# Weaving background steps twice per weight chunk, with scores and transposes of p in separate steps

## The chip, the core and the metric

One core of a Trainium2 chip runs one encoder block on 512 tokens of width 1024. The metric is the device time of the core in microseconds (us). The engines are named as in the profile: PE is TensorE (PEld its weight loads), DVE is VectorE, ACT is ScalarE, POOL is GpSimd, SP is SyncE.

## What is computed

One layer: a half-step SwiGLU, a mixer that joins a two-way RG-LRU with a neighbourhood attention, an output projection, and a second half-step SwiGLU. All of it is float32. The part around the change is the mixer:

```python
x = x + FFN_RES * _swiglu(_rmsnorm(x, norm_ffn1), w_ffn1_gu, w_ffn1_down)
h = _rmsnorm(x, norm_mix)
xr, gr, q, k, v, ga, gb = jnp.split(h @ w_in, splits, axis=-1)
xc = _centred_dwconv(xr, conv_w, conv_b)
y_lru = (rglru_forward(xc) + rglru_backward(xc)) * jax.nn.gelu(gr)
q = _rmsnorm(q, q_norm) * HEAD_DIM ** -0.5        # per head of 64
k = _rmsnorm(k, k_norm)
y_att = _neighbourhood_attention(q, k, v, rel_pos_bias)   # 8 x 16 window on an 8 x 64 grid
x = x + (sigmoid(ga) * y_lru + sigmoid(gb) * y_att) @ w_out
x = x + FFN_RES * _swiglu(_rmsnorm(x, norm_ffn2), w_ffn2_gu, w_ffn2_down)
```

## The kernel before

Every float32 product is made of three matmuls on operands that are cut into a high and a low part: high by high, high by low, low by high (`mm3`, and the same three lines in `tok_group`). Weights come in chunks of 128 x 1024 (`load_w`): SP issues the load, ACT casts the high part (L120), DVE subtracts to get the low part (L123), both with high priority. A chunk feeds 24 matmuls of 512 columns.

The mixer runs as one stream of such chunks: 8 for the LRU input (`xr`), then six token groups of 4 chunks (q, k, v of heads 0 to 7, then q, k, v of heads 8 to 15; `tok_group`), then 24 chunks of gates in three families of 8 (`gates`), then 8 chunks of the output projection. These streams accumulate in the four PSUM banks of the pool `acc`.

Everything else of the mixer is background work in two lanes of Python generators. `lanes["lru"]` holds two RG-LRU jobs (`lru`, four tiles of 128 channels each). `lanes["att"]` holds two attention jobs (`heads(0)` and `heads(1)`, eight heads each). `weave(rate)` adds a rate to a lane's account and emits one step of the generator for each whole unit in it. It is called once behind each chunk, with the rates of `RATE` for the stage: "xr", "t0" (first three token groups), "t1" (next three, when `heads(0)` is in the lane), "g" (gates, when `heads(1)` has been added). `until` empties a lane as far as a gate needs it.

A job of `heads` has these steps: the root and reciprocal of the q and k norms (L755, L756); the scaling of q (L761); the scaling of k (L761); `start(0)`, which transposes the first q and k tiles (L770, L772); then ten steps i = 0 to 9 over eight units (four pairs of heads, two halves each). Step i emits `scores` of unit i (12 matmuls L796 into two PSUM tiles of the pool `aux`; DVE adds the bias and takes the maximum, L806; ACT takes the exponential, L809; DVE scales, L815), for odd i from 3 on `apply` of an earlier pair (32 matmuls L834), for even i up to 4 `start` of the next pair, and then `turn` of unit i-1: eight transposes of p (L823), four into each of two `aux` tiles, which ACT copies out (L825). The pool `aux` has four PSUM banks. `scores` takes two, `start` two, each half of `turn` one and `apply` one; the LRU gates use them too.

The order within each engine's queue is made by a planner from the program: the program's order is the priority, and an instruction whose inputs its model finds ready may go ahead of earlier ones that are not. `after(i, prev)` tells it to place i behind prev; it makes no wait on the chip.

Of the kernel before, what the change touches and what calls it, by code (L numbers as in the profile page):

```python
# [11 lines left out]
AF = mybir.ActivationFunctionType  # L12
# [7 lines left out]
KT = D // P  # L20
# [38 lines left out]
ATT_LAG = 1, 2  # L59

RATE = {
    "xr": {"lru": 4, "att": 0.0},
    "t0": {"lru": 3, "att": 0.0},
    "t1": {"lru": 2, "att": 0.75},
    "g": {"lru": 3, "att": 0.75},
}


# [1 line left out]
def block_kernel(ctx: ExitStack, tc, a, out):  # L70
    nc = tc.nc
# [7 lines left out]
    dram = ctx.enter_context(tc.tile_pool(name="dram", bufs=1, space=bass.MemoryType.DRAM))  # L79

    uid = [0]

    def nm(s):
        uid[0] += 1
        return f"{s}_{uid[0]}"
# [3 lines left out]
    def big_t(dt=F32, shape=(P, T), n="b"):  # L89
        return big.tile(list(shape), dt, tag="big", bufs=NBIG, name=nm(n))  # L90

    def pair_t():
        return big.tile([P, 2, T], F32, tag="pair", bufs=4, name=nm("pair"))

    def acc_t():
        return acc.tile([P, T], F32, tag="acc", name=nm("acc"))
# [37 lines left out]
    def load_w(src, n, act=True):  # L134
        raw = raw_t()
        H, L = hl_t()
        s = slice(0, n)
        ld = nc.sync.dma_start(raw[:, s], src[:, s])
        if nld[0] < 8:
            tc.keep_in_program_order(ld)  # L140
        nld[0] += 1
        with tc.high_priority():
            split(raw[:, s], H[:, s], L[:, s], act)
        return H, L

    def mm3(ps, wh, wl, xh, xl, first, last, skip=False):
        nc.tensor.matmul(ps, wh, xh, start=first, stop=False, skip_group_check=skip)  # L147
        nc.tensor.matmul(ps, wh, xl, start=False, stop=False, skip_group_check=skip)  # L148
        nc.tensor.matmul(ps, wl, xh, start=False, stop=last, skip_group_check=skip)  # L149

    def feat_chunk(src, nk, xh, xl, ps, k0, ktot, act=True):
        H, L = load_w(src, nk * P, act)
        for k in range(nk):
            s = slice(k * P, (k + 1) * P)
            kk = k0 + k
            mm3(ps, H[:, s], L[:, s], xh[kk], xl[kk], kk == 0, kk == ktot - 1)


    def make_xg(gcol, tag):
        xh, xl = [], []  # L160
        for k in range(KT):
            xh.append(xpool.tile([P, T], F32R, tag=f"xh{k}", name=nm("xh")))
            xl.append(xpool.tile([P, T], F32R, tag=f"xl{k}", name=nm("xl")))
        ssum = xpool.tile([P, T], F32, tag="ssum", name=nm("ssum"))

        def one(k):
            g = small[:, gcol + k : gcol + k + 1]
            x = xres[k]
            nc.scalar.activation(xh[k], x, AF.Copy, scale=g)
            return nc.vector.scalar_tensor_tensor(xl[k], x, g, xh[k].bitcast(F32), ALU.mult, ALU.subtract)  # L170

        def square(k):
            x = xres[k]
            if k == 0:
                nc.scalar.activation(ssum, x, AF.Square)
            else:
                sq = big_t(n="xsq")
                nc.scalar.activation(sq, x, AF.Square)
                nc.vector.tensor_tensor(ssum, ssum, sq, ALU.add)

        return xh, xl, ssum, one, square
# [24 lines left out]
    def after(i, prev):  # L206

        i, prev = getattr(i, "ins", i), getattr(prev, "ins", prev)
        tc.add_manual_dep(i, prev.name, mybir.DependencyInfo(
            mybir.DependencyClass.NoSync, mybir.DependencyReason.DATA), reason="order")  # L210


    mark = {}

    def sub(out_, in0, in1, neg=False):

# [271 lines left out]
    def weave(rate):  # L488
        for ln, n in rate.items():
            q = lanes[ln]  # L490
            due[ln] += n
            while due[ln] >= 1 and q:
                try:
                    next(q[0])
                    due[ln] -= 1
                except StopIteration:
                    q.pop(0)
            if not q:
                due[ln] = 0.0
# [6 lines left out]
    xh, xl, ssum, one, square = make_xg(C_G1, "a")  # L506
# [53 lines left out]
    xh, xl, ssum = nxt["v"][:3]  # L560
# [45 lines left out]
    def conv(f, ps, r):  # L606
        xp = big.tile([P, T + 4], F32, tag="xp", bufs=2, name=nm("xp"))
        nc.gpsimd.memset(xp[:, 0:2], 0.0)
        nc.gpsimd.memset(xp[:, T + 2 : T + 4], 0.0)
        with tc.high_priority():  # L610
            nc.vector.tensor_tensor(perm(xp[:, 2 : T + 2]), blk(ps), blk(r), ALU.mult)
        y = big_t(n="xc")
        w = lambda k: small[:, C_CW + f * 4 + k : C_CW + f * 4 + k + 1]
        nc.scalar.activation(y, xp[:, 0:T], AF.Identity, scale=w(0), bias=small[:, C_CB + f : C_CB + f + 1])
        for k in range(1, CONV_W):
            mark["xr"] = nc.vector.scalar_tensor_tensor(y, xp[:, k : k + T], w(k), y, ALU.mult, ALU.add)
        xc[f] = y
# [61 lines left out]
    rb = None  # L679
    for f in range(KT):  # L680
        ps = acc_t()
        feat_chunk(a["wxr"][f], KT, xh, xl, ps, 0, KT)
        if f == 0:
            rb, rcol, vx = rstd(ssum)
            epsv = const.tile([P, NCB], F32, name="epsv")
            nc.vector.tensor_scalar(epsv, vx, EPS, None, ALU.mult)
        conv(f, ps, rb)
        weave(RATE["xr"])
        if (f + 1) % LRU_F == 0:
            lanes["lru"].append(lru(range(f + 1 - LRU_F, f + 1)))  # L690
# [4 lines left out]
    def tok_group(w, hf):  # L695
        pss = [acc_t() for _ in range(NCB)]
        for kp in range(4):
            H, L = load_w(a["wqkv"][w * 2 + hf, kp], 1024)
            for j in range(NCB):
                tj = slice(j * P, (j + 1) * P)  # L700
                for k in range(2):
                    kk = kp * 2 + k
                    s = slice(k * T, (k + 1) * T)
                    nc.tensor.matmul(pss[j], xh[kk][:, tj], H[:, s], start=kk == 0, stop=False)  # L704
                    nc.tensor.matmul(pss[j], xl[kk][:, tj], H[:, s], start=False, stop=False)  # L705
                    nc.tensor.matmul(pss[j], xh[kk][:, tj], L[:, s], start=False, stop=kk == KT - 1)  # L706
            if kp < 3:
                weave(RATE[phase[0]])
        return pss
# [31 lines left out]
    def bias(g):  # L741

        for hp in range(2):
            bms[g, hp] = tiny.tile([P, 3, 2 * P], F32, tag="bm", bufs=4, name=nm("bm"))
            ld = nc.gpsimd.dma_start(bms[g, hp], a["rpb"][g * 2 + hp])
            if g == 0:
                after(ld, mark["xr"])

    def heads(hf, raws, st):

        rq = tiny.tile([P, 2, NCB, 8], F32, tag="rq", name=nm("rq"))
        for w in range(2):
            for j in range(NCB):
                nc.vector.tensor_scalar(rq[:, w, j, :], st[:, w, j, :], 1.0 / HD, epsv[:, j : j + 1], ALU.mult, ALU.add)
        nc.scalar.activation(rq, rq, AF.Sqrt)  # L755
        nc.vector.reciprocal(rq, rq)  # L756
        yield
        for w in range(2):
# [93 lines left out]
        for i in range(len(units) + LC):  # L852
            if i < len(units):
                fi, n2 = units[i]
                last = scores(fi, n2)
                if i >= LC and units[i - LC][1]:
                    apply(units[i - LC][0], last)
                if n2 == 0:
                    if fi < 3:
                        start(fi + 1)  # L860
                    if hf * 4 + fi + 1 < KT:
                        bias(hf * 4 + fi + 1)
            if 0 <= i - LB < len(units):
                for hp in range(2):
                    turn(*units[i - LB], hp)
            if len(units) <= i < len(units) + LC and units[i - LC][1]:
                apply(units[i - LC][0])
            yield

    att = [None] * KT  # L870
    phase = ["t0"]
# [9 lines left out]
    def gates(w, fs, fn, scale=1.0):  # L881
        q = [pair_t() for _ in range((len(fs) + 1) // 2)]
        for i, f in enumerate(fs):
            ps = acc_t()
            feat_chunk(a["wg3"][w * KT + f], KT, xh, xl, ps, 0, KT, f % 2 == 0)
            with tc.high_priority():
                nc.vector.tensor_tensor(q[i // 2][:, i % 2], ps, rb, ALU.mult)
            weave(RATE[phase[0]])
        for i, t in enumerate(q):
            n = min(2, len(fs) - 2 * i)  # L890
            nc.scalar.activation(t[:, :n], t[:, :n], fn, scale=scale)
        return [(f, q[i // 2][:, i % 2]) for i, f in enumerate(fs)]
# [13 lines left out]
    for fs in GB_BATCH:  # L906
        for f, t in gates(2, fs, AF.Tanh, 0.5):
# [4 lines left out]
            L = big_t(F32R, n="yl")  # L912
# [9 lines left out]
    for m in range(KT):  # L922
        nc.sync.dma_start(xres[m], xd[m])
        ps = acc_t()
# [10 lines left out]
    xh, xl, ssum = nxt["v"][:3]  # L935
# [84 lines left out]
```

## Time and profile before

| | |
|---|---|
| median of 3 runs | 1131.18 us (1131.16 to 1131.39) |
| profiled execution | 1131.25 us, span 1129.1 us |
[...]
| PE busy | 1122.3 us (99% of the span) |
| DVE, ACT, POOL busy | 837.7, 594.0, 19.2 us |
| mixer stage | about 358 to 787 us of the span |

Busy time says that an engine had something in it. As matmuls are pipelined, a busy PE can still lose time between the starts of two matmuls. So the places of loss are read from the start times of a timeline of PE, and what caused them from the timelines of DVE and ACT at the same place.

### The profile page before, as it was taken

How to read it: one execution, taken by the hardware profiler on the slowest of the kernel's cores; microseconds unless marked ns; L12 is line 12 of the kernel's file. 1: busy time of each engine (PE TensorE's matmuls, PEld its weight loads, DVE VectorE, ACT ScalarE, POOL GpSimd, SP SyncE). 2: the span in 40 equal slices, each digit the busy share in tenths (PEclk: the TensorE clock that was granted, in tenths of full speed). 3: DMA queues.
4: the chain of work that ended last, by engine and by line, in shares of the span. 5: the costliest groups of instructions: out<-in, count | busy, mean ns of one | idle time of the engine just before them, and what ended most of it. 6: DMA issues, size and time to landing. Idle time of an engine off the chain costs nothing.

```text
span 1129.1 us, 17245 instructions
## 1 busy us (share of the span) xinstructions
PE 1122.3 (99%) x6867; PEld 992.8 (88%) x6867; DVE 837.7 (74%) x1294; ACT 594.0 (53%) x896; POOL 19.2 (2%) x52
## 2 busy tenths in 40 slices
PE   9999999999999999999999999999999999999998
PEld 7899999988888888888788888888999999998887
DVE  7888888894736798797865576858688888894552
ACT  8554554563624595985564254656445445464340
POOL 0000000000000000010110000000000000000000
PEclk9999999999999999999999999999999999999999
DMA  8242333443433342353453332355133333253321
GB/s 267 90 130 77 116 109 95 133 142 99 131 93 112 94 159 84 113 162 103 133 155 103 93 104 84 111 170 187 56 90 118 94 110 115 90 170 96 130 76 38
DMA packets 43697, 130.69 MB, mean 116 GB/s; under 512 B 5984, under 2 KB 8544, under 8 KB 43616
## 3 DMA queue, kind: packets, MB, share of 16 engines
q1 hardware_dynamic: 39744, 119.36, 33.6%
q0 software_dynamic: 3296, 9.97, 2.8%
q8 instruction: 54, 0.88, 0.3%
q10 hardware_dynamic: 576, 0.26, 0.1%
q14 instruction: 27, 0.22, 0.1%
HBM read 121.17 MB, written 8.39 MB: 115 GB/s over the span
## 4 chain that ended last, share of the span: by engine, by line
PE 97%; DVE 1%; ACT 1%; issue 0%; DMA 0%; ACTq 0%; DVEq 0%
PE acc L267 29%; PE acc L147 11%; PE acc L148 11%; PE acc L149 11%; PE aux L267 5%; PE aux L147 4%; PE aux L148 4%; PE aux L149 4%; PE acc L705 4%; PE acc L704 4%; PE acc L706 4%; PE aux L823 1%; PE aux L834 1%; PE aux L796 1%; PE acc L380 1%; PE acc L382 1%
## 5 line engine op out<-in xcount | busy, mean ns | idle before, releaser
L120 ACT ACTIVATE wh<-wraw 128x1024 fp32r<-128x1024 f32 (+3 forms) x242 | 240.9, 999 | 331.8 <-PE acc L267 95.9
L123 DVE TENSOR_TENSOR wl<-wraw,wh 128x1024 fp32r<-128x1024 f32 (+3 forms) x254 | 291.3, 1150 | 137.2 <-ACT wh L120 136.6
L267 PE MATMUL acc<-s,wh 128*128 128x256 f32 x1216 | 220.5, 283 | 0.0
L267 PEld LDWEIGHTS acc<-s,wh 128*128 128x128 f32 x1216 | 189.7, 192 | 0.0
L267 PE MATMUL acc<-s,wl 128*128 128x256 f32 x608 | 172.1, 283 | 0.0
L147 PE MATMUL acc<-xh,wh 128*128 128x512 f32 x304 | 120.1, 395 | 0.0
L148 PE MATMUL acc<-xl,wh 128*128 128x512 f32 x304 | 119.0, 392 | 0.0
L149 PE MATMUL acc<-xh,wl 128*128 128x512 f32 x304 | 118.9, 391 | 0.0
L267 PEld LDWEIGHTS acc<-s,wl 128*128 128x128 f32 x608 | 116.7, 192 | 0.0
L267 PE MATMUL acc<-xh,wl 128*128 128x256 f32 x304 | 86.0, 283 | 0.0
L267 PE MATMUL acc<-xl,wh 128*128 128x256 f32 x304 | 86.0, 283 | 0.0
L267 PE MATMUL acc<-xh,wh 128*128 128x256 f32 x304 | 86.0, 283 | 0.0
L704 PE MATMUL acc<-wh,xh 128*128 128x512 f32 x192 | 75.2, 392 | 0.0
L705 PE MATMUL acc<-wh,xl 128*128 128x512 f32 x192 | 74.8, 390 | 0.0
L706 PE MATMUL acc<-wl,xh 128*128 128x512 f32 x192 | 74.8, 389 | 0.0
L301 DVE TENSOR_TENSOR wraw<-wraw,pair 128x1024 f32<-128x1024 f32 x57 | 69.6, 1220 | 0.8
L147 PE MATMUL aux<-hh,wh 128*128 128x512 f32 (+1 forms) x181 | 69.9, 386 | 0.0
L148 PE MATMUL aux<-hl,wh 128*128 128x512 f32 (+1 forms) x181 | 69.9, 386 | 0.0
L149 PE MATMUL aux<-hh,wl 128*128 128x512 f32 (+1 forms) x181 | 69.9, 386 | 0.0
L149 PE MATMUL acc<-hh,wl 128*128 128x512 f32 (+1 forms) x176 | 67.9, 386 | 0.0
L148 PE MATMUL acc<-hl,wh 128*128 128x512 f32 (+1 forms) x176 | 67.9, 386 | 0.0
L147 PE MATMUL acc<-hh,wh 128*128 128x512 f32 (+1 forms) x176 | 67.9, 386 | 0.0
(203 smaller groups left out, 2196.9 us busy)
## 6 DMA issues: line engine op xcount, KB each, us to landing
wraw<-wqkv SPq DMA_DIRECT2D x24, 512.0 KB, 3.6
wraw<-wg SPq DMA_DIRECT2D x24, 512.0 KB, 3.6
wraw<-w1d SPq DMA_DIRECT2D x22, 512.0 KB, 3.6
wraw<-w2d SPq DMA_DIRECT2D x22, 512.0 KB, 3.6
pair<-w2s SPq DMA_DIRECT2D x20, 512.0 KB, 3.6
wraw<-w2s SPq DMA_DIRECT2D x20, 512.0 KB, 3.6
wraw<-w1s SPq DMA_DIRECT2D x18, 512.0 KB, 3.7
pair<-w1s SPq DMA_DIRECT2D x18, 512.0 KB, 3.6
```

What stands on the lines that cost most here:

```text
L120: nc.scalar.activation(H, raw, AF.Copy)
L123: nc.vector.tensor_tensor(L, raw, H.bitcast(F32), ALU.subtract)
L147: nc.tensor.matmul(ps, wh, xh, start=first, stop=False, skip_group_check=skip)
L148: nc.tensor.matmul(ps, wh, xl, start=False, stop=False, skip_group_check=skip)
L149: nc.tensor.matmul(ps, wl, xh, start=False, stop=last, skip_group_check=skip)
L267: nc.tensor.matmul(o, w_[:, c], x_, start=first and m + k == 0 and w_ is H and x_ is xh_, stop=m + k == 4 and w_ is L, skip_group_check=True)
L301: nc.vector.tensor_tensor(t, t, o, ALU.add)
L380: nc.tensor.matmul(pre[i], w[i][1][:, s], xh[k], start=k == 0, stop=False)
L382: nc.tensor.matmul(pre[i], w[i][1][:, s], xl[k], start=False, stop=False)
L704: nc.tensor.matmul(pss[j], xh[kk][:, tj], H[:, s], start=kk == 0, stop=False)
L705: nc.tensor.matmul(pss[j], xl[kk][:, tj], H[:, s], start=False, stop=False)
L706: nc.tensor.matmul(pss[j], xh[kk][:, tj], L[:, s], start=False, stop=kk == KT - 1)
```

## The change

The rates of the LRU lane are halved, and `weave` is called a second time in the middle of each chunk of the mixer's stream: behind half of the k steps of a chunk in `feat_chunk` (new argument `mid`, given for the xr chunks and the gates), and behind two of the four token blocks in `tok_group`. The rate of the attention lane stays at 0.75 per call, so it is doubled per chunk. In `heads` a `yield` is put between `scores` (with `apply` or `start`) and `turn`, so that each of the ten steps becomes two. The root of the q and k norms is placed behind the last matmul that was emitted before it (`mark["mm"]`).

```diff
 RATE = {
-    "xr": {"lru": 4, "att": 0.0},
-    "t0": {"lru": 3, "att": 0.0},
-    "t1": {"lru": 2, "att": 0.75},
-    "g": {"lru": 3, "att": 0.75},
+    "xr": {"lru": 2, "att": 0.0},
+    "t0": {"lru": 1.5, "att": 0.0},
+    "t1": {"lru": 1, "att": 0.75},
+    "g": {"lru": 1.5, "att": 0.75},
 }
...
-        nc.tensor.matmul(ps, wl, xh, start=False, stop=last, skip_group_check=skip)
+        mark["mm"] = nc.tensor.matmul(ps, wl, xh, start=False, stop=last, skip_group_check=skip)
...
-    def feat_chunk(src, nk, xh, xl, ps, k0, ktot, act=True):
+    def feat_chunk(src, nk, xh, xl, ps, k0, ktot, act=True, mid=None):
...
             mm3(ps, H[:, s], L[:, s], xh[kk], xl[kk], kk == 0, kk == ktot - 1)
+            if mid is not None and k == nk // 2 - 1:
+                weave(mid)
...
-        feat_chunk(a["wxr"][f], KT, xh, xl, ps, 0, KT)
+        feat_chunk(a["wxr"][f], KT, xh, xl, ps, 0, KT, mid=RATE["xr"])
...
-                    nc.tensor.matmul(pss[j], xh[kk][:, tj], L[:, s], start=False, stop=kk == KT - 1)
+                    mark["mm"] = nc.tensor.matmul(pss[j], xh[kk][:, tj], L[:, s], start=False, stop=kk == KT - 1)
+                if j == 1:
+                    weave(RATE[phase[0]])
...
-        nc.scalar.activation(rq, rq, AF.Sqrt)
+        after(nc.scalar.activation(rq, rq, AF.Sqrt), mark["mm"])
...
                     if hf * 4 + fi + 1 < KT:
                         bias(hf * 4 + fi + 1)
+            yield
             if 0 <= i - LB < len(units):
                 for hp in range(2):
                     turn(*units[i - LB], hp)
...
-            feat_chunk(a["wg3"][w * KT + f], KT, xh, xl, ps, 0, KT, f % 2 == 0)
+            feat_chunk(a["wg3"][w * KT + f], KT, xh, xl, ps, 0, KT, f % 2 == 0, RATE[phase[0]])
```

## Rows read from the trace of the kernel before

**Rows 1.** The page: busy time, share of the span and instructions of each engine.
```profile
PE 1122.3 (99%) x6867; PEld 992.8 (88%) x6867; DVE 837.7 (74%) x1294; ACT 594.0 (53%) x896; POOL 19.2 (2%) x52
```

**Rows 2.** Waits of PE's weight loads: who for whom, total us, times, longest.
```profile
PEld aux L823 <- DVE nmx L806: 2.6, 4, 1.0
```

**Rows 3.** Timeline: start, us, engine, line, out<-in, count; late transposes of p.
```profile
547.18 0.39 PE L704 MATMUL acc<-wh,xh 128*128 128x512 f32 x1
548.15 0.66 PE L823 MATMUL aux<-ident,p 128*128 128x128 f32 x4 [0.58 <-DVE nmx L806]
...
673.13 0.39 PE L147 MATMUL acc<-xh,wh 128*128 128x512 f32 x1
673.63 0.66 PE L823 MATMUL aux<-ident,p 128*128 128x128 f32 x4
...
696.29 0.40 PE L149 MATMUL acc<-xh,wl 128*128 128x512 f32 x1
696.93 0.66 PE L823 MATMUL aux<-ident,p 128*128 128x128 f32 x4 [0.24 <-DVE nmx L806]
...
727.74 1.46 PE L823 MATMUL aux<-ident,p 128*128 128x128 f32 x8
...
735.49 0.42 PEld L834 LDWEIGHTS aux<-PT,v 128*64 128x64 f32 x8 [0.17 <-issue]
```

**Rows 4.** Timeline of DVE ahead of the first of them.
```profile
543.17 1.90 DVE L761 TENSOR_TENSOR qk<-qk,rq 128x512 f32<-128x512 f32 x3
...
546.19 1.22 DVE L123 TENSOR_TENSOR wl<-wraw,wh 128x1024 fp32r<-128x1024 f32 x1
547.32 0.42 DVE L806 CUSTOM_DVE_ANT_0 so<-aux,bm 128x256 f32<-128x256 f32 x1
```

**Rows 5.** Timeline of ACT ahead of that: two table loads.
```profile
541.00 1.28 ACT L755 ACT_TABLE_LOAD   x1
...
542.57 1.28 ACT L809 ACT_TABLE_LOAD   x1
```

**Rows 6.** Timeline of PE: scores, apply and transposes of p in one detour.
```profile
553.21 0.39 PE L705 MATMUL acc<-wh,xl 128*128 128x512 f32 x1
553.43 0.39 PE L706 MATMUL acc<-wl,xh 128*128 128x512 f32 x1
553.75 0.39 PE L796 MATMUL aux<-kh,qh 64*128 64x256 f32 x2
...
554.67 0.66 PE L834 MATMUL aux<-PT,v 128*64 128x128 f32 x8
...
556.57 1.09 PE L823 MATMUL aux<-ident,p 128*128 128x128 f32 x8
```

**Rows 7.** Timeline of PE: transposes of p in a detour of their own.
```profile
608.24 1.03 PE L823 MATMUL aux<-ident,p 128*128 128x128 f32 x8
609.03 0.48 PE L147 MATMUL acc<-xh,wh 128*128 128x512 f32 x1
609.34 0.40 PE L148 MATMUL acc<-xl,wh 128*128 128x512 f32 x1
```

**Rows 8.** Busy time of each engine in two stretches (us and instructions).
```profile
463.00:473.00 10.00, 10.00 (x46) 8.29 (x45) 10.00 (x16) 9.99 (x15) 0.00 (x0) 1.00 0.35 109
...
500.00:511.00 11.00, 11.00 (x50) 9.09 (x50) 11.00 (x13) 6.82 (x10) 0.00 (x0) 1.00 0.29 96
```

**Rows 9.** Timelines of PE and DVE: the first q and k tiles, transposed and split.
```profile
517.95 0.60 PE L770 MATMUL aux<-ident,qk 128*128 128x128 f32 x4
...
520.81 0.74 DVE L779 SCALAR_TENSOR_TENSOR kl<-aux,small,kh 128x512 fp32r<-128x512 f32 x1
```

**Rows 10.** Timelines of DVE and PE at the start of the output projection.
```profile
735.59 1.23 DVE L123 TENSOR_TENSOR wl<-wraw,wh 128x1024 fp32r<-128x1024 f32 x1 [0.17 <-ACT wh L120]
...
737.60 0.50 PE L147 MATMUL acc<-yh,wh 128*128 128x512 f32 x1
...
740.51 0.69 DVE L123 TENSOR_TENSOR yl<-pair,yh 128x512 fp32r<-128x512 f32 x1 [0.76 <-ACT yh L120]
```

More of the change, by code (lines that the diff above doesn't have):

```diff
@@ L81, in block_kernel @@
     uid = [0]
+    mark = {}
     def nm(s):
@@ L210, in after @@
             mybir.DependencyClass.NoSync, mybir.DependencyReason.DATA), reason="order")
-    mark = {}
     def sub(out_, in0, in1, neg=False):
```

## The prediction

> **What bounds the kernel.** I read the page's busy times first. [...] So PE's own queue sets the end, and the change, which neither adds nor removes a matmul, can gain only what PE loses between matmuls. The view of waits names the one repeated loss of the mixer: PE's weight loads wait 2.6 us, in 4 places, for the DVE work L806 before transposes of p [rows 2]. The timeline of PE then shows what that costs in starts. In the stream, one 512-column matmul follows another after 0.22 to 0.23 us (553.21 to 553.43) [rows 6]; I use 0.227. What exceeds it is lost.
>
> **Where the loss lies** [rows 3]. Transposes of p start 0.97 us after the matmul ahead of them at 548.15 (0.74 lost), 0.50 at 673.63 (0.27 lost) and 0.64 at 696.93 (0.41 lost). At 727.74 eight transposes take 1.46 instead of the 1.09 of an undisturbed block [rows 6]: 0.37. At 735.49 the last apply has nothing in front of it but its own transposes and waits about 0.18. The sum is 0.74 + 0.27 + 0.41 + 0.37 + 0.18 = 1.97 us.
>
> **Why they are late.** A score step holds two aux banks, and with a start in the same step all four. The transposes that follow in the same step need a bank that DVE frees with L806. At 547.3 DVE comes to L806 only after three scalings L761 (1.90 us) and a weight split (1.22) [rows 4]. Those scalings are there because the root of the second half's norms ran at 541.0, ahead of its place, between two exponentials; it also cost ACT two table loads of 1.28 us [rows 5].
>
> **Part 1: a yield between scores and transposes.** The transposes now come half a chunk later, 12 matmuls or 12 x 0.227 = 2.7 us. The worst delay shown is 0.74 us, and transposes that were ready at 548.15 would not be asked for before 549 or so, as the detour with their scores ended at about 546.4. So the four waits on L806 go, and so does the one at 735.49, because the attention lane ends early (part 3). Gain 1.97. Three of the late blocks were also cut into two groups of four, with a few stream matmuls between; each group enters and leaves the stream by itself. From their start times I estimate 0.07 to 0.17 for each cut, 0.4 in all. These go too: gain 0.4.
>
> The price is more detours. In a joint detour, scores begin 0.32 us after the last stream matmul (0.09 over the beat) and take 0.92, apply takes 1.90, and the transposes come next [rows 6]. Transposes by themselves enter without loss and take 0.79 to the next stream matmul, and the second stream matmul comes after 0.31 (0.08 to 0.09 lost) [rows 7]. A score detour with no transposes behind it is not in the trace. If it leaves like rows 7, a cut adds one exit, 0.09, and saves some of what the transposes lose behind another kind of matmul. Bounds are 0 and 0.10 per cut, I take 0.05. Ten of the sixteen transposing steps were joint and are now cut (the other six were already apart in the queue): 10 x 0.05 = +0.5, bounds 0 and +1.0.
>
> **Part 2: twice per chunk.** The LRU lane keeps its pace per chunk: 2 x 2 for 4, 2 x 1.5 for 3, 2 x 1 for 2. Its matmuls are 512 columns wide like the stream's and fit in at the same beat, so where they are put costs nothing; ACT and DVE work hides under PE as before. I set 0, bounds -0.4 to +0.4 for the few 0.1 us hitches of first uses.
>
> **Part 3: the attention lane.** It has 4 + 20 steps for 4 + 10, at 1.5 per chunk for 0.75. The units keep their pace (two steps per unit), but the four opening steps take 2.7 chunks for 5.3. So each job runs about 2.7 chunks (some 14 us) ahead; the first scores are step 5, due at the seventh call (5 / 0.75 = 6.7), so `heads(0)` has them 3.5 chunks after it is added rather than 7, and `heads(1)` ends some 4 chunks before the gates do. Two things become tight. **First scores:** they now have their place half a chunk after start(0), 0.8 + 2.7 = 3.5 us after its first transpose; the split k that they need was done 521.55 - 517.95 = 3.6 us after it [rows 9]. So PE may wait 0 to 1.2 us (one weight split of 1.22 in between [rows 4]), twice; I take 0.1 each, as the trace's distance is only 0.1 too long: +0.2. **The output projection:** it began at 737.60 behind the last detour, and its last input was split by 741.2; its eighth k step is due after 21 matmuls, 4.8 us, at 742.4 [rows 10]. Without that detour it begins about 2.9 us earlier (1.90 + 0.79 and the losses beside them [rows 6, 7]). The last gate then needs two ACT and four DVE passes, at the 0.69 of the last of them about 4.1 us with no hand-overs, and may meet a weight split of 1.23 [rows 10]. Against 4.8 to 5.0 us of cover that is 0 to 0.7 late; I take +0.1.
>
> **Part 4: the root in its place.** For `heads(1)` it leaves the stretch at 541 to 548 and runs when the exponentials of `heads(0)` are over. For `heads(0)` it moves from about 461 to about 495, with 8 scalings of 0.63 (a third of the 1.90 us [rows 4]) and a reciprocal of some 0.5: about 5.6 us of DVE work go from a stretch where DVE is full (10.00 of 10) to one where DVE is full too (11.00 of 11) [rows 8]. PE was 100% busy in both, so a full DVE by itself costs PE nothing; behind these scalings queue the LRU scans, which nobody needs until the gates. I set 0, bounds 0 to +5.6, the upper one if all of it got in front of the first scores' chain. The two table loads at 541 took 1.28 us each, with only 0.29 us for the root between their end and start (542.28 to 542.57) [rows 5]. [...]
>
> **Sum:** -1.97 - 0.4 + 0.5 + 0.2 + 0.1 = -1.57 us. The profiled execution took 1131.25 us, 0.07 over the median, so 1131.25 - 1.57 = 1129.7, and against the median 1129.6.
>
> **The rivals.** What a measurement of this kernel can tell from no change is about 0.2%, 2.26 us: below 1128.92 is faster, above 1133.44 slower.
>
> A, the forecast: 1129.6, with a spread of 1128.8 to 1130.6 from the bounds of parts 1 to 3. Chance 0.55.
>
> B, the waits come back elsewhere: aux still has four banks, a score step with a start still fills all four, and DVE frees them no earlier. The first scores, and steps where a split and an evacuation stand in front of L806, lose what the late transposes lost: -1.57 + 1.6 gives 1131.2, between 1130.4 and 1132.5. This includes the case that the planner puts the transposes back to where they were. For it: all waits name L806. Against it: 2.7 us more distance than waits of 0.74. Chance 0.20. [...]
>
> C, slower: the DVE stretch from 489 to 511 is the place. It holds hardly any slack [rows 8] and gets 5.6 us of scalings while the scores arrive 3.5 chunks earlier. It decides when more than 2.7 us of other DVE work stands between a score block and its L806. Then the transposes wait in PE's queue with the stream behind them, and PE pays up to the 5.6 us that were moved: 1129.6 + 5.6 = 1135.2. Against it: PE lost nothing at 500 to 511 with DVE full. Chance 0.10.
>
> D, better than the forecast: cuts cost nothing and neither tight place waits: 1131.18 - 2.4 = 1128.8. Chance 0.15.
>
> **How the numbers follow.** The likeliest is A, 1129.6. D and the low end of A (0.05) are faster: 0.20. C is slower: 0.10. The rest is the same: 0.70. The range 1128.6 to 1132.0 holds A, D and most of B and leaves out C and the end of B.
>
> **What would show it.** Right: no wait of PE on L806; transposes of p always in blocks of eight, with 0.79 us to the next stream matmul; score detours by themselves at 1.1 us (0.09 + 0.92 + 0.09) over the beat; one Sqrt table load after the last exponential of `heads(0)`; the last apply some 20 us before the projection. Wrong: PE idle before L796 in 500 to 515, before L147 in the first chunk of the projection, or a score detour that costs more than 1.2. A change of more than 3 us either way would mean that something outside these detours moved.

## The result, and the profile after

The changed kernel takes 1135.86 us (median of 6 runs, 1135.18 to 1136.11) and the kernel before 1131.13 beside it on the same chip: a ratio of 1.0041 [1.0031, 1.0051], slower by 4.7 us. The forecast was 1129.6, with a range up to 1132.0, so it was wrong in sign and missed the range. The profiled execution took 1135.99 us with a span of 1134.2, 4.7 and 5.1 us more than before: outside the span, before its first or behind its last instruction, lie 2.1 us before and 1.8 after.

The page's busy times after, to be held against [rows 1]. In the new kernel scores are L802, transposes of p L829, bias and maximum L812, exponentials L815, apply L840, the casts of a start L782 and L784 on ACT, L783 and L785 on DVE, the evacuation of q and k L723.

```profile
PE 1124.4 (99%) x6867; PEld 994.9 (88%) x6867; DVE 837.7 (74%) x1294; ACT 589.4 (52%) x892; POOL 19.4 (2%) x52
```

The view of waits of PE after (tile and line that waited, who for: total us, times, longest), to be held against [rows 2]:

```profile
PE aux L829 <- DVE ql L783: 4.1, 1, 4.1
PE aux L116 <- DVE pol L582: 1.1, 1, 1.1
```

The waits on the maximum (L806 in [rows 2], here L812) are gone, all of them, in the view of the weight loads too. One new wait of 4.1 us has come, and it names the low part of the next q tile, L783. (The 1.1 us for L116 lie in the first microseconds of the kernel, and before has them too.)

PE's timeline at that place (start, us, engine, line, tile, shape, count, wait):

```profile
509.54 0.39 PE L710 MATMUL acc<-wl,xh 128*128 128x512 f32 x1
509.86 0.39 PE L802 MATMUL aux<-kh,qh 64*128 64x256 f32 x2
...
510.56 0.29 PE L802 MATMUL aux<-kh,ql 64*128 64x256 f32 x2
514.96 1.09 PE L829 MATMUL aux<-ident,p 128*128 128x128 f32 x4 [4.10 <-DVE ql L783]
515.69 0.78 PE L708 MATMUL acc<-wh,xh 128*128 128x512 f32 x1
516.27 0.63 PE L709 MATMUL acc<-wh,xl 128*128 128x512 f32 x1
516.69 0.63 PE L710 MATMUL acc<-wl,xh 128*128 128x512 f32 x1
...
519.68 0.47 PE L708 MATMUL acc<-wh,xh 128*128 128x512 f32 x1
519.99 0.39 PE L709 MATMUL acc<-wh,xl 128*128 128x512 f32 x1
```

Two losses stand here. From 510.57 (the last matmul of the scores that begin at 510.56) to 514.96 PE starts nothing, about 4.3 us more than a matmul of scores needs. And the ten stream matmuls from 515.69 to 519.99 take 4.30 us where ten beats of 0.227 are 2.27; the beat is 0.43. With the four transposes ahead of them, which take 0.74 us (514.96 to 515.69) instead of the 0.35 of the four at 525.91 (to 526.26), and less the 0.09 that the return to the stream costs in [rows 7], that is 2.3 us. The windows of this stretch say why (PE, PEld, DVE, ACT and POOL busy, granted clock, DMA share, GB/s):

```profile
505.00:510.00 5.00, 4.87 (x34) 3.80 (x34) 5.00 (x14) 2.53 (x6) 0.00 (x0) 1.00 0.26 98
510.00:515.00 5.00, 0.90 (x13) 0.71 (x14) 5.00 (x11) 4.94 (x11) 0.00 (x0) 0.80 0.01 2
515.00:522.00 7.00, 7.00 (x23) 5.75 (x24) 7.00 (x15) 3.14 (x8) 0.00 (x0) 0.65 0.27 75
522.00:529.00 7.00, 7.00 (x34) 5.67 (x33) 6.32 (x16) 3.64 (x9) 1.14 (x2) 1.00 0.62 190
```

PE's granted clock fell while PE stood still. Windows of 1 us give 1.00 up to 513, 0.51 for 513 to 514, 0.50 for each of the five from 514 to 519, 0.58 for 519 to 520 and 1.00 for 520 to 521. A clock of 0.80 over 5 us and 0.65 over 7 makes 2.0 and 4.9 us at 0.50. The mean granted clock of the profiled execution is 0.997, that of the kernel before 1.000. DVE is full to 522 (5.00 of 5 and 7.00 of 7 us), as in [rows 8].

So 4.3 + 2.3 = 6.6 us were lost within ten microseconds. All the rest gained: 4.7 - 6.6 = -1.9 us, of which 0.3 lie outside the span.

**What PE waits for.** Scores(0) and start(1) at 504.8 to 506.9 hold all four aux banks. Scores(1) at 509.86 get the two that DVE's L812 freed by 508.4. The transposes of p need a third, and that is freed only when L783 has read the q tile of start(1).

In the program neither scores(1) nor these transposes stand here: scores(1) come behind the first chunk of the next group, the transposes half a chunk later. The planner put scores(1) and half of the transposes directly behind the group's last matmul; 36 stream matmuls (515.69 to 525.68) follow before the other half. Why it did so no run shows; that the next group's accumulators were not free in its model is the likeliest reason.

Two starts of PE in the group's fourth chunk, and ACT's timeline ahead of the wait:

```profile
501.86 0.48 PE L708 MATMUL acc<-wh,xh 128*128 128x512 f32 x1
...
503.09 0.39 PE L710 MATMUL acc<-wl,xh 128*128 128x512 f32 x1
```

```profile
507.46 1.28 ACT L815 ACT_TABLE_LOAD   x1 [4.20 <-DVE nmx L812]
508.75 0.51 ACT L815 ACTIVATE p<-so,nmx 128x256 f32<-128x256 f32 x1
...
510.25 1.04 ACT L123 ACTIVATE wh<-wraw 128x1024 fp32r<-128x1024 f32 x1
511.19 0.49 ACT L815 ACTIVATE p<-so,nmx 128x256 f32<-128x256 f32 x1
...
511.69 0.67 ACT L782 ACTIVATE qh<-aux,gq 128x512 fp32r<-128x512 f32 x1
512.26 0.67 ACT L784 ACTIVATE kh<-aux,small 128x512 fp32r<-128x512 f32 x1
512.83 0.58 ACT L723 ACTIVATE qk<-acc 128x512 f32<-128x512 f32 x1
```

and DVE's:

```profile
505.16 1.88 DVE L668 TENSOR_TENSOR gate<-gate,th 128x512 f32<-128x512 f32 x3
506.96 0.41 DVE L812 CUSTOM_DVE_ANT_0 so<-aux,bm 128x256 f32<-128x256 f32 x1
...
508.34 1.21 DVE L676 TENSOR_TENSOR_SCAN th<-gate,gate 128x512 f32<-128x512 f32 x1
509.48 1.19 DVE L674 TENSOR_TENSOR_SCAN th<-gate,gate 128x512 f32<-128x512 f32 x1
510.59 0.66 DVE L677 TENSOR_TENSOR th<-th,th 128x512 f32<-128x512 f32 x1
...
511.25 1.19 DVE L676 TENSOR_TENSOR_SCAN th<-gate,gate 128x512 f32<-128x512 f32 x1
...
512.88 1.21 DVE L126 TENSOR_TENSOR wl<-wraw,wh 128x1024 fp32r<-128x1024 f32 x1
...
514.09 0.72 DVE L783 SCALAR_TENSOR_TENSOR ql<-aux,gq,qh 128x512 fp32r<-128x512 f32 x1
```

The row to notice is L723 at 512.83. The last matmul of the group of q, heads 8 to 15, started at 509.54, so its four accumulators were complete by 510. The first of them was complete long before, with the sixth matmul of the fourth chunk (503.09 + 0.39, about 503.5). Their evacuation, the work that lets the stream go on, stands in ACT's queue behind a table load, four exponentials, a weight cast and two casts of start(1). ACT sat idle for 4.20 us before 507.46 and still did not take the first accumulator: what was emitted in the middle of the fourth chunk has its place ahead. L723 came 9.3 us after the first accumulator was complete, behind all of that. Without the transposes in front, the stream would still have waited for the first copy, until 512.83 + 0.58 = 513.41, which by estimate is 2.5 of the 4.1 us.

The same work elsewhere costs what was forecast. A detour is attention work of PE between two stream matmuls. Scores with apply and transposes by themselves, one of six such pairs (before, [rows 6], in one detour):

```profile
540.21 0.39 PE L802 MATMUL aux<-kh,qh 64*128 64x256 f32 x2
...
542.50 0.61 PE L840 MATMUL aux<-PT,v 128*64 128x128 f32 x8
...
545.91 1.04 PE L829 MATMUL aux<-ident,p 128*128 128x128 f32 x8
```

By PE's start times (from the stream matmul ahead of the detour to the second one behind it, less two beats) the first costs 3.02 us, transposes alone 0.88 to 0.89, scores alone 1.11 to 1.13, and the joint detour of before 3.85.

### The profile page after: what moved, and what is told of

It is laid out like the page before. It is cut to its first block, busy times and chain, and to the rows that moved or that the text cites. A ratio compares the mean times of both kernels' runs of the same rounds, so it can differ in the third digit from the quotient of the medians.

```text
span 1134.2 us, 17233 instructions
## 1 busy us (share of the span) xinstructions
PE 1124.4 (99%) x6867; PEld 994.9 (88%) x6867; DVE 837.7 (74%) x1294; ACT 589.4 (52%) x892; POOL 19.4 (2%) x52
## 4 chain that ended last, share of the span: by engine, by line
PE 97%; DVE 1%; DMA 1%; ACT 0%; issue 0%; ACTq 0%
PE acc L271 29%; PE acc L150 11%; PE acc L151 11%; PE acc L152 11%; PE aux L271 5%; PE aux L151 4%; PE aux L152 4%; PE aux L150 4%; PE acc L708 4%; PE acc L710 4%; PE acc L709 4%; PE aux L840 1%; PE aux L829 1%; PE aux L802 1%; PE acc L386 0%; PE acc L388 0%
## 5 line engine op out<-in xcount | busy, mean ns | idle before, releaser
L150 PEld LDWEIGHTS acc<-xh,wh 128*128 128x128 f32 x304 | 57.1, 188 | 12.6 <-issue 1.0
```

## The experiments

Five theories were set against each other; their letters are those of the expectations.
- **E**: the mid call in the fourth chunk of a token group emits attention work ahead of the group's evacuations, and ACT's queue holds the stream up.
- **C**: the cause that the prediction's rival C named: the root's place moves 5.6 us of scalings into the full DVE.
- **L**: the early opening alone is enough, as the attention starts while the second RG-LRU job still scans.
- **D**: the wait needs both, the order of E and a DVE that is full with work that nobody waits for (scans of the second RG-LRU job), so that a start's banks come free late.
- **P**: the tiles of the SBUF pool run out, as two jobs' tiles now overlap.

Each run is told beside the kernel before on the same chip (medians 1131.12 to 1131.26). Outside the span lie 2.1 us in the kernel before, e8 and e10, and 1.8 in all other kernels; no run shows why, and 0.3 us of a difference can be that.

### The mid call of the fourth chunk (E)

In `tok_group`:

```diff
-                if j == 1:
+                if j == 1 and kp < 3:
                     weave(RATE[phase[0]])
```
with a second `weave` at the end of `qk_raw` and of `v_get`, so that the number of calls stays.

> The changed kernel, but in the token groups the call in the middle of the fourth chunk is made behind the evacuation of the group instead (two calls there). Rates and the root stay as in the change. Theory E (evacuation behind the scores): in the changed kernel the middle call of the fourth chunk of q (heads 8 to 15) puts the first scores, their exponentials and the next start ahead of the copies L723 in ACT's queue; ACT waits there for DVE, the accumulators are not freed, and PE's queue brings scores and transposes that wait too. With the evacuation first, the wait of about 4.3 us at 510 and the 6.8 us at the lower clock are gone: 1129.0 to 1129.8. Theory C (DVE too full because the scaling of q and k was moved into 494 to 501): the work on DVE is the same, PE still waits 3 to 4 us there: 1134 to 1136. Theory L (attention starts while the second RG-LRU job still scans): the first scores come only half a chunk later, most of the wait stays: 1132 to 1136.

Measured 1131.75 us, 1.0010 [1.0000, 1.0019]: 4.1 of the 4.7 us are gone. ACT's timeline has the first evacuation here:

```profile
503.51 0.60 ACT L723 ACTIVATE qk<-acc 128x512 f32<-128x512 f32 x1 [0.26 <-PE acc L710]
```

and PE's timeline the transposes that follow scores(1), here in the program's order, behind 24 stream matmuls, scores(1) and 12 more:

```profile
518.95 0.66 PE L831 MATMUL aux<-ident,p 128*128 128x128 f32 x4
521.36 0.63 PE L831 MATMUL aux<-ident,p 128*128 128x128 f32 x4 [1.75 <-DVE kl L787]
```

The evacuation waits for nothing but the group's last matmuls, the stream goes on between the scores (514.89) and their transposes, and the granted clock stays at 1.00 from 510 to 529 in the profiled execution. But the second half of the transposes still waits 1.8 us for a bank of start(1), behind a weight split of 1.22. E holds the larger part, not all of it: the time is above the 1129.0 to 1129.8 that E alone expected. Three of the ten executions took 1133.1 to 1133.7 at a mean granted clock of 0.998, the other seven 1131.4 to 1131.9 at 0.999 or 1.000.

### The root's place (C)

```diff
-        after(nc.scalar.activation(rq, rq, AF.Sqrt), mark["mm"])
+        nc.scalar.activation(rq, rq, AF.Sqrt)
```
in the changed kernel; and, the other way round, the root's place alone in the kernel before.

> The changed kernel without the ordering of the root of the q and k norms (the planner may run it early again); everything else as changed. Theory C: the scaling of q and k goes back to before 475, DVE has 5.6 us less to do in 489 to 511, the wait goes: 1129.0 to 1130. Theory E: the queue of ACT still has the exponentials and casts ahead of L723, so the wait stays, smaller by what DVE is earlier: 1 to 4 us of wait, 1131 to 1135.5. Theory L: as E.

> The kernel before with nothing but the root of the q and k norms in its place. By the steps of the prediction the wait at 548 (0.8 us with its cut block) goes and nothing comes: 1130.2 to 1130.8. Theory C (moving 5.6 us of DVE work into the full stretch costs by itself): 1132 to 1136. No effect: 1131.1.

Measured: without the root's place 1136.88, 1.0050 [1.0035, 1.0065]; with it alone 1130.75, 0.9997 [0.9988, 1.0006]. The first has the waits at the same place in two portions (2.1 us for L829 and 1.7 for L776, both `<- DVE ql L783`) and the clock falls again: the stream matmuls from 510.06 to 511.48 follow one another after 0.42 to 0.57 us, and the mean granted clock is 0.998. So the moved scalings are not the cause, and C falls in its cause. (1136.88 lies a little above E's range too.)

The second holds a surprise for the prediction's reading of [rows 4]. The root no longer runs at 541, the scalings are out of this stretch, and the transposes are late all the same: they start 0.885 us after the matmul ahead instead of 0.97. DVE's timeline of that kernel:

```profile
545.14 1.23 DVE L124 TENSOR_TENSOR wl<-wraw,wh 128x1024 fp32r<-128x1024 f32 x1
546.28 0.42 DVE L806 CUSTOM_DVE_ANT_0 so<-aux,bm 128x256 f32<-128x256 f32 x1
```

The weight split stands in front of L806 as in [rows 4], and both come about 1.05 us earlier. But the order now has one stream matmul between start and transposes instead of four, so the transposes wait nearly as long. By PE's starts the whole place, scores included, costs 3.46 us instead of 3.64: the scalings accounted for about 0.2 of what is lost there. And none of the 0.4 us of this run lies inside the span, which is 1129.0 (median) for both kernels.

### The pool (P), and a slow opening

> The changed kernel with 52 instead of 48 buffers of 128 x 512 in the shared pool. Theory P (the copies L723 come late because no buffer is free while the RG-LRU holds its tiles): they come earlier, the wait shrinks to under 1 us: 1129 to 1131. Theories E, C and L: the order of the queues around the wait is the same, the wait stays at 4 us with the low clock behind it: 1135 to 1136.5.

```diff
-NBIG = 48
+NBIG = 52
```

Measured 1135.63, 1.0044 [1.0027, 1.0061], with the same wait of 4.1 us for L783. P falls.

> The changed kernel with an empty step behind each of the four opening steps of an attention job (root, q scaling, k scaling, first start), so that the first scores come at 5.3 chunks, as before the change, and not in the middle of the fourth chunk of q. Theory L: the wait goes, 1129 to 1130. Theory E: it goes as well, as no scores stand ahead of that evacuation. Theory C: DVE still gets the scaling at 494 to 501, but no scores follow: it goes too. What this run tells: if the wait stays, all three are wrong. The attention now ends with the last gate as before, so 0.2 us of wait in the last detour may come back: 1129.2 to 1130.2.

Here an empty step stands behind each of the four opening steps:

```diff
         start(0)
         yield
+        yield
```

Measured 1132.45, 1.0012 [1.0002, 1.0021], above the 1129.2 to 1130.2 expected. The wait of 4 us is gone, as the scores fall elsewhere; but they have their place half a chunk behind a start, and wait there:

```profile
PE aux L804 <- DVE kl L787: 0.9, 1, 0.9
```

That is the wait of the prediction's part 3, which set 0 to 1.2 us with 0.1 as its value: [rows 9] was the right measure, and the upper end the right value: the detour costs 3.10 us instead of 1.94. The rest of the excess stands in other detours (at 565.44, transposes and scores in one cost 2.88 instead of 0.88 + 1.11).

### The work in front of the bank (D)

The changed kernel without the eight scans and the four sums of the second RG-LRU job: 8 x 1.2 + 4 x 0.66, about 12 us of DVE.

```diff
-                nc.vector.tensor_tensor_scan(h, av, ix, 0.0, ALU.mult, ALU.add)
+                if fs[0] == 0:
+                    nc.vector.tensor_tensor_scan(h, av, ix, 0.0, ALU.mult, ALU.add)
```
and the same for the backward scan and the sum.

> The changed kernel without the eight scans and four sums of the second RG-LRU job (12 us of DVE work between about 490 and 525 are left out, and with them that part of the result). The order of PE's queue around the wait is the same: scores, half a transpose block, then the stream. Theory D (the wait needs both, the evacuation behind the exponentials in ACT's queue and a DVE that is full with scans): the wait of 4.3 us shrinks to under 1.5 us, PE's clock stays at its upper level there, 1129.0 to 1132.5. Theory E alone (ACT's order is enough): the wait stays at 3 us or more and the clock falls, 1134 to 1136.

Measured 1132.59, 1.0013 [1.0004, 1.0023]. PE's timeline, which has the same order of work as after:

```profile
510.36 0.29 PE L804 MATMUL aux<-kh,ql 64*128 64x256 f32 x2
513.04 0.63 PE L831 MATMUL aux<-ident,p 128*128 128x128 f32 x4 [2.40 <-DVE ql L785]
513.43 0.48 PE L710 MATMUL acc<-wh,xh 128*128 128x512 f32 x1
```

What frees the bank, on ACT and DVE:

```profile
510.88 0.67 ACT L784 ACTIVATE qh<-aux,gq 128x512 fp32r<-128x512 f32 x1
...
511.01 1.23 DVE L126 TENSOR_TENSOR wl<-wraw,wh 128x1024 fp32r<-128x1024 f32 x1
...
512.15 0.74 DVE L785 SCALAR_TENSOR_TENSOR ql<-aux,gq,qh 128x512 fp32r<-128x512 f32 x1
```

The wait is 2.40 instead of 4.10, between the under 1.5 that D expected and the 3 or more of E alone, and the granted clock stays at 1.00 from 505 to 529 in this execution (the beat behind is 0.23). So 1.7 of the 4.1 us come from DVE's scans. What is left is ACT's queue, where the cast of q still ends only at 511.55, and behind it a weight split on DVE; how the 2.4 us divide between the two no run shows. The median mixes two kinds of executions: five took 1131.8 to 1132.1 at a mean granted clock of 1.000, five 1133.1 to 1133.5 at 0.998. By that the clock falls in some executions and not in others, and the fall costs about 1.4 us; the kept trace is of an execution without it. In the changed kernel, with its wait of 4.1 us, it fell to 0.50 in the execution whose trace we have.

### Each part alone

> The kernel before with nothing but the yield between scores and transposes, and twice the attention rate (1.5 per call, one call behind each chunk), so that the units keep their pace and the opening steps are as early as in the change. The call of the fourth chunk is behind the evacuation. Theory E: no wait of 4 us; the late transposes of the kernel before go, small waits for DVE in 500 to 525: 1129.5 to 1131.5. Theory L (the early opening alone is enough): a wait of 3 us or more, 1133 to 1136.

The kernel before, with one call per chunk as it was:

```diff
-    "t1": {"lru": 2, "att": 0.75},
-    "g": {"lru": 3, "att": 0.75},
+    "t1": {"lru": 2, "att": 1.5},
+    "g": {"lru": 3, "att": 1.5},
...
+            yield
             if 0 <= i - LB < len(units):
```

Measured 1133.11, 1.0018 [1.0008, 1.0028]: slower by 2.0 us. The early opening alone brings waits: scores that wait for L806 at 515.43 (1.96 us where 1.11 to 1.13 are usual), and a start for which all four banks are taken:

```profile
524.30 0.29 PE L796 MATMUL aux<-kh,ql 64*128 64x256 f32 x2
526.03 0.66 PE L770 MATMUL aux<-ident,qk 128*128 128x128 f32 x4 [1.45 <-ACT PT L825]
```

At 1.5 steps per call two steps sometimes fall into one call, here transposes, then scores with a start, and no stream matmul stands between them. No wait of 4 us comes: the early opening alone (L) is not enough for it, though it was worse than E expected here (1129.5 to 1131.5).

> Only the second call in the middle of each chunk, with both lanes at half rate (attention 0.375 per call); no yield between scores and transposes, root as in the kernel before. Theories E and D together (scores ahead of the evacuations of a group, in front of a full DVE): the attention lane keeps the pace of before, the first scores come some three chunks after the group with the evacuations, so no wait over 1 us between 500 and 525, no fall of the clock, and the late transposes of before mostly stay: 1130.5 to 1131.5. Rival: the mid calls alone put work between the evacuations and cost a wait of 4 us wherever the pace: 1134 or more.

The kernel before with the mid calls of the diff alone and no `yield`, the attention lane too at half rate:

```diff
+    "t1": {"lru": 1, "att": 0.375},
+    "g": {"lru": 1.5, "att": 0.375},
```

Measured 1129.97, 0.9991 [0.9982, 1.0000]. No wait over 1 us between 500 and 525. The late transposes stay (0.75, 0.28 and 0.41 us lost at 544.95, 673.38 and 696.67), as expected; the one of 727.74 is gone. The starts of this trace show 0.65 us of the gain (the projection begins at 736.95 for 737.60), and 0.3 lie outside the span.

The single parts change the time by -0.4 (root), +2.0 (yield) and -1.2 us (mid calls), +0.4 together; all at once it is +4.7. By spans it is 0.0, +2.3 and -0.8, +1.5 together, for +5.1. The rest is what none of them does alone: early scores from the one meet a call ahead of the evacuations from the other.

### Does the forecast hold without the wait?

```diff
         start(0)
         yield
+        for _ in range((5, 1)[hf]):
+            yield
```

Five empty steps behind the first start of the first job, one in the second, put the first scores back to 523.6 (e12), about where the kernel before has them (524.37). e8 and e10 have this on top of e1's edit, e11 also leaves the root free, and e12 has it alone, with the mid call in the fourth chunk as in the changed kernel.

> The changed kernel with the call of the fourth chunk of a token group behind the evacuation, and empty steps behind the first start (five in the first attention job, one in the second), so that the first scores come as late as before the change, after the scans, and not half a chunk behind the first start. If the waits were the whole loss, what is left is what the prediction counted: 1131.1 less 1.9 of detours and waits and 0.6 of the RG-LRU's hitches, 1128.6, between 1128.3 and 1129.6. If the change has another cost: 1130 or more.

> The same kernel as e8_late_scores with more rounds: the changed kernel, without the mid call in the fourth chunk of a token group (two calls behind the evacuations), five empty steps ahead of the first start of the first job and one in the second. If the terms of the forecast are right and only the wait at 510 was missed: 1129.4, ratio 0.9985 with an interval that leaves out 1. Rival: the gain of e8 was chance, and it comes out within 0.05% of before.

> As e10, with the root as in the kernel before (free to be put earlier). If the root's place brings what it brought alone (0.4 us): 1129.8. If it brings nothing here, as no transposes are late any more: the same as e10 within 0.2 us. If the root in its place is what made e8 quick: 1131.

> The changed kernel with all its calls, the mid call in the fourth chunk of a token group among them; only five empty steps are put behind the first start of the first job and one behind that of the second, so that no scores are due in the fourth chunk of the second k group. If what costs is that scores and a start stand in ACT's queue ahead of that group's evacuations: no wait over 0.5 us between 500 and 525, the clock stays, 1129.3, as e10. If the mid call of the fourth chunk costs by itself whatever it emits, or if the transposes that follow are late anywhere behind a full DVE: 1131 to 1134, with waits over 1 us.

(The group meant is that of q, heads 8 to 15.)

Measured:

| kernel | median us | before | ratio |
|---|---|---|---|
| e8 | 1129.40 | 1131.13 | 0.9985 [0.9976, 0.9995] |
| e10, the same kernel | 1129.30 | 1131.14 | 0.9985 [0.9977, 0.9994] |
| e11, root free | 1129.05 | 1131.14 | 0.9982 [0.9973, 0.9991] |
| e12, the pause alone | 1129.12 | 1131.26 | 0.9981 [0.9972, 0.9990] |

All four beat both kernels. The root adds nothing once transposes have their distance (e11 is 0.25 us under e10, and by spans both take 1127.2). The mid call in the fourth chunk costs nothing by itself (e12); it costs when it has scores to emit. e12 doesn't tell E from L and D, since its scores also come when the scans are over; e1, e5 and e7 do. All of its waits of PE:

```profile
PE aux L116 <- DVE pol L582: 1.1, 1, 1.1
PE aux L271 <- ACT wh L123: 0.9, 1, 0.9
PE acc L384 <- DVE wh L369: 0.3, 1, 0.3
```

and ACT's timeline where the changed kernel had L723 only at 512.83:

```profile
502.35 0.68 ACT L787 ACTIVATE kh<-aux,small 128x512 fp32r<-128x512 f32 x1
503.31 0.60 ACT L723 ACTIVATE qk<-acc 128x512 f32<-128x512 f32 x1 [0.28 <-PE acc L710]
```

No wait of the mixer is left in the list; the three end in the first 64 us of the kernel.

## Why the prediction was wrong

**The step that failed** is in part 1, "the transposes now come half a chunk later, 12 matmuls", together with part 3's price of 0.1 us for the first scores. A step counts half a chunk only where the stream has matmuls to put between. At a group's end it has none until ACT has evacuated the accumulators, and there the planner let scores(1) and the first half of the transposes of the same step follow one another directly: no matmul where 12 were counted, and a wait of 4.1 us. Nothing in the prediction asked what a call in the middle of the fourth chunk puts ahead of L723 in ACT's queue. That was visible in the kernel before: the evacuation is emitted behind the whole group, and [rows 8] shows DVE full exactly when part 3 brings the first scores to it, 3.5 chunks earlier. Part 3 sized only the wait for the split k (it came too: the detour at 504.77 costs 2.35 us instead of 1.94). The term of 0.2 us measured 6.6 at this one place, 4.3 of waiting and 2.3 of clock.

**Rivals.** Rival C gave 1135.2, close to the measured time and in the right stretch, but its hit is in part luck. Its condition, more than 2.7 us of other DVE work between scores and their L806, did not hold: between scores(0), which end at 506, and L812 at 506.96 stood three L668 of 1.88 us. The work stood in front of L783, so the bank was that of the start, not that of the scores; rival B's sentence, that a score step with a start fills all four banks, was the more exact half. The price came out by another sum, 4.3 us of waiting and 2.3 of clock, and the cause it named, the moved scalings, was refuted by e2 and e6. "PE lost nothing at 500 to 511 with DVE full" was poor evidence against C: before, PE's stream there depended on DVE only for the weight splits, which have priority, and the change made scores and transposes depend on it too. As for B, e12 has no wait of the mixer left in its list with no aux bank added, so here more distance was enough; no run adds an aux bank.

**What was right, by e12.** Its 38 detours from 480 to 800 cost 55.3 us, the 31 of before 57.1: -1.8, and the sum for them was -1.97 - 0.4 + 0.5 = -1.87. By pieces:
- Late transposes and cut blocks: the five places lost 0.81, 0.44, 0.58, 0.36 and 0.20 against undisturbed detours, 2.4 in all, for 2.37 forecast. But two groups of four that enter without a wait cost 0.89 together, as much as eight (0.88): the 0.4 was lateness too, not the cutting.
- A cut between scores and transposes costs 3.02 + 0.89 - 3.85 = 0.06 with an apply and 1.12 + 0.88 - 1.955 = 0.05 without, 0.05 forecast.
- Part 2 was set to 0; the mixer's first token group starts 0.56 us sooner in the changed kernel (408.59 for 409.15), 0.12 of which it had already when the mixer began. Of the four hitches of 0.1 us at the first RG-LRU matmuls (383.7 to 395.2) one is left, so the bound of -0.4 was the value.
- The projection lost 0.25 us in the changed kernel (two matmuls behind 747.31 that start 0.14 and 0.11 late), 0.1 forecast.
- Part 4: the root's place was set at 0, and alone measured -0.4 (e6), which the interval can't tell from 0.

**The signs that were named.** "No wait on L806" came true and said too little, as the wait moved to another bank. "Transposes always in blocks of eight" failed at 514.96, where four came alone. "PE idle before L796 in 500 to 515" was set down as a sign of being wrong, and it showed (0.4 us at 504.77), beside the far larger one five microseconds later. The last apply came 24 us before the projection, for some 20 forecast.

**Of the table loads**, one shows at 507.46 above: it takes 1.28 us, as the two in [rows 5] do, and an exponential starts 1.29 us after its start.

## What to carry to other kernels

Before you put background work into the middle of a unit of the main stream, write down for each engine what is emitted behind it, above all what frees the stream's own accumulators. Here that stood in ACT's queue behind a table load, four exponentials and three casts, and came 9.3 us after the first accumulator was complete. A distance counted in steps holds only where the main engine has something to do in between; at the end of the group here 12 matmuls became none. And a full engine that costs nothing now (PE busy for 11.00 of 11 us beside a full DVE in [rows 8]) is no proof of slack: after the change PE waited 4.1 us for that engine. Ask what will depend on it.

## What the runs showed of the hardware

In the profiled execution of the changed kernel PE waited 4.1 us. The granted clock was still 1.00 from 512 to 513, fell to 0.50 within the wait and was back at 1.00 by 520, some 6.9 us in all, which cost 2.3 us of matmuls on top of the wait. In e4, with the same wait of 4.1 us, the windows give 0.99 and 0.77:

```profile
510.00:515.00 5.00, 1.10 (x13) 0.78 (x12) 5.00 (x10) 4.90 (x10) 0.00 (x0) 0.99 0.00 0
515.00:522.00 7.00, 6.79 (x26) 5.67 (x27) 7.00 (x14) 2.87 (x7) 0.00 (x0) 0.77 0.26 76
```

If the clock was at 0.50 there too, that is some 3.3 us (0.01 x 5 and 0.23 x 7, over 0.5), and by 6.79 us of busy PE x 0.23 an estimated cost of 1.6.

In e1 and e5, whose profiled executions wait 1.8 and 2.4 us at a granted clock of 1.00, the executions of one kernel fell into two groups some 1.4 to 1.9 us apart in time and 0.998 against 1.000 or 0.999 in mean clock. So the wait of 4.1 us in the changed kernel has a price in two parts, 4.3 us of standing still and 2.3 of clock behind it. What decides between the two groups, and how long the clock stays down, can't be told from these runs.
